# Shifted S5 kernel tables, gate stores from ScalarE, and tied TensorE steps in a hybrid S5 / SSD / DeltaNet layer

## The chip, the cores and the metric

The program runs on one core of one Trainium2 chip. The metric is the device time of one execution in microseconds (us), the median of several runs on fast executions. The core has five engines with queues of their own: TensorE (PE in the profile; its weight loads are PEld), VectorE (DVE), ScalarE (ACT), GpSimd (POOL) and SyncE (SP). Each queue is worked in order: an instruction that waits holds up all that stand behind it on its engine. Transfers between memory and the on-chip buffers are issued by a queue (here nearly all by SP) and carried by 16 DMA engines.

## The reference

One layer with 1024 channels is applied to 128 context tokens and 256 latent tokens with shared weights. The kernel keeps activations transposed, 8 blocks of 128 channels by 384 tokens.

```python
h = rmsnorm(x, g0) * (1 + sc1) + sh1                     # sh, sc, gate = silu(cond) @ ada_w + ada_b
x = x + 0.5 * g1 * swiglu(h, ffn_wi[0], ffn_wo[0])       # first feed-forward, width 2816
h = rmsnorm(x, g1) * (1 + sc2) + sh2
proj = h @ w_in          # u_s5, z, xbc, dt, qkv, beta, a, dn_gate, gate_raw
# S5: diagonal complex recurrence per channel group, forward and backward, then a GLU
# SSD: Mamba-2 chunks of 128;  DeltaNet: chunked delta rule with a triangular inverse
merged = sum(sigmoid(gate_raw[i]) * branch[i] for i in range(3))
x = x + g2 * (merged @ w_out)
h = rmsnorm(x, g2) * (1 + sc3) + sh3
x = x + 0.5 * g3 * swiglu(h, ffn_wi[1], ffn_wo[1])
y = rmsnorm(x, final_g)
```

## The kernel before

All dense products are done in three passes. `split_w` (L279) loads a 512 KB weight block into `wraw` (three buffers), ScalarE rounds it to `whi` (L284), VectorE makes the remainder `wlo` (L285; two buffers each), and `mm3` (L288) runs, for each of 8 slices of the contraction, `whi` with the high part of the activation, `whi` with its low part and `wlo` with the high part: 24 matmuls of 384 columns for one block of 128 outputs.

The order on every engine is made at build time by a scheduler that plays the program through with its own times; the program text and the limits of buffers bound it. `tc.issue_after(x)` sets a lower bound: what is written under it is issued after instruction `x`.

The stages in order of time are: the first feed-forward (`ffn(0)`), in whose gaps the modulation rows (`ada_rest`) and the S5 tables (`s5_tables`) are made; the mixer; the second feed-forward. In the mixer:

- Four S5 input blocks (`dense_in(0..3)`) are multiplied with the unnormalised activation `xh`, `xl`. `rstd_bcast` (L320) sums squares on TensorE (L326), takes the root on VectorE, and multiplies it back out to all partitions (L333); ScalarE copies this to `rb` (L337). Everything after needs `rb`: the blocks' scaling (L748), the normalised activation `hh`, `hl` (`modnorm`, L366), and a block of small scalars (`wsm`).
- The S5 input goes through memory (`dU`) and comes back in chunks of eight tokens as `UU` (eight transfers, L769). `chunk_inputs(b)` (L772), for b = 0 to 7, loads a table `sw` and runs 8 small matmuls (L778) whose results ScalarE copies to `Ss` (L781 to L783).
- Eighteen blocks of the DeltaNet and SSD inputs follow (`dense_in`, `conv`), then the z gate in four weight loads (L876 to L878, 36 matmuls of 256 columns for three tiles each half).
- The S5 scan over chunks, 31 steps on VectorE (L825, L826, L829), starts when all of `Ss` stands, and its end is copied to `Hc` (L952 to L955).
- The S5 output (L975) takes for each j of 8 the tables `ew` (one 512 KB transfer, L962) and, for even j, `tw`. `tw` holds for each of eight positions s the S5 kernel shifted by 16 s columns. Memory holds the kernel unshifted as `dK`, rows of 240 columns, and eight transfers of 64 KB (L966) read eight shifted pieces. `sw`, `ew`, `tw` and two later tiles share three buffers (`w4`).
- `gates()` (L1007) yields the dense filler of the inverse part: 16 gate blocks whose tanh is stored to `dM` (L1012), and steps of `ada_cols` (L234), each half of which loads modulation columns (L241) and multiplies them (L243). It is woven with `inv16` (L921), which inverts 16 by 16 blocks on VectorE and passes them through memory (`U`, L929; `dI`, L942), and then with the inverses and recurrences.

Of the kernel before, what the change touches and what calls it, by code (L numbers as in the profile page):

```python
# [10 lines left out]
F32 = mybir.dt.float32  # L11
# [9 lines left out]
P = 128  # L21
# [17 lines left out]
GK = ()  # L39
NSC = 0  # L40
NEARLY = (0, 0, 2, 1, 2)
NYF = 3
# [10 lines left out]
TW = T + 2  # L53
# [87 lines left out]
def tile_hybrid(ctx: ExitStack, tc: tile.TileContext, a, o):  # L141
    nc = tc.nc
# [136 lines left out]
    def split_w(dram, nk, w=P, into=None):  # L279
# [6 lines left out]
        return hi, lo  # L286

    def mm3(pt, w, xh, xl, k0, nk, start, stop):  # L288
        hi, lo = w
        for k in range(nk):  # L290
            PE.matmul(pt, hi[:, k, :], xh[k0 + k], start=start and k == 0, stop=False)  # L291
            PE.matmul(pt, hi[:, k, :], xl[k0 + k], start=False, stop=False)  # L292
            PE.matmul(pt, lo[:, k, :], xh[k0 + k], start=False, stop=stop and k == nk - 1)  # L293

# [25 lines left out]
    def rstd_bcast(acc, width, copy=True, ps=None, rest=(), root=False):  # L320
# [11 lines left out]
        for t in range(3):  # L332
            PE.matmul(pb[:, t * P:t * P + P], y[:, t:t + 1].to_broadcast([P, P]), ident, start=True, stop=True)  # L333
        if not copy:
# [114 lines left out]
    dE = dram.tile([8, P, 2, 2, 2, P], F32, name="dE")  # L449
    dK = dram.tile([4, 2, 4, 32, 240], F32, name="dK")  # L450
    dU = dram.tile([512, 8, 48], F32, name="dU")
# [97 lines left out]
    def s5_tables(sp, b, bb, craw, pq, pb):  # L549
# [50 lines left out]
        S.copy(kc[:, 128:240], pf[:, 16:128])  # L600
        nc.sync.dma_start(out=dK[b % 4, b // 4].rearrange("g i c -> (g i) c"), in_=kc)
        yield
# [92 lines left out]
    def mixer(es, xv, acc, xh, xl, sc):  # L695
# [46 lines left out]

        pts = [dense_in(m, xh, xl, TW) for m in range(2)]
        rb = rstd_bcast(acc, D)
        for m in range(4):
            pt = pts[m] if m < 2 else dense_in(m, xh, xl, TW, psD if m < 3 else psC)
            ur = t2("ur", None)[:, 0:T]
            V.tensor_tensor(ur, pt[:, 0:T], rb, op=ALU.mult)  # L748
            bu = shifts(pt)
            us = wk.tile([P, 8, 48], F32, name="us", tag="sgate", bufs=NSG)  # L750
            for e, s0, s1 in HALVES:
                S.activation(us[:, :, s0 // 8:s1 // 8], ur[:, s0:s1].rearrange("p (c s) -> p s c", s=8),
                             AF.Identity, bias=bu[:, e:e + 1])
            nc.sync.dma_start(out=dU[m * P:m * P + P], in_=us)
# [34 lines left out]
        for which, tokt in ((1, ktok), (0, qtok), (2, vtok)):  # L789
            for m in range(4):  # L790
# [6 lines left out]
                if which < 2:  # L797
                    sq = raw
                    S.activation(sq, pt.rearrange("p a b -> p (a b)"), AF.Square)
                    V.tensor_reduce(ss[:, which, :, m], sq.rearrange("p (a b) -> p a b", b=P), axis=AX.X, op=ALU.add)  # L800
                if which == 0:
                    chunk_inputs(2 * m)
                    chunk_inputs(2 * m + 1)
        V.tensor_scalar(ss, ss, EPS, None, op0=ALU.add)
# [153 lines left out]
        gsh, gsl = blocks("gsh", 4, FR), blocks("gsl", 4, FR)  # L958
        dk = dK.rearrange("b q g i c -> b i (q g) c")
        for j in range(8):  # L960
            ew = w4("ew").rearrange("p q (r g) c -> p q r g c", r=2)
            nc.sync.dma_start(out=ew, in_=dE[j])  # L962
            if j % 2 == 0:
                tw = w4("tw")
                for s in range(8):
                    nc.sync.dma_start(out=tw[16 * s:16 * s + 16].rearrange("p q g c -> p (q g) c"),  # L966
                                      in_=dk[j // 2, 0:16, :, 16 * (7 - s):16 * (7 - s) + P])
                pt = psB([P, 4, P])
# [38 lines left out]
        def gates():  # L1007

            cols = chain(*(ada_cols(s, lambda: wk.tile([P, 256], F32, name="arow")) for s in TSEC))
            for n in (2, 1):  # L1010
                for m in range(KD):
                    nc.sync.dma_start(out=dM[m, n], in_=gate(n, m))  # L1012
                    next(cols, None)
                    yield
# [138 lines left out]
        for d in range(2):  # L1153
            G.memset(hss[d], 0.0)
            for g in range(2):
                nc.sync.dma_start(out=hss[d][H2[g], 256 * g:256 * g + 256], in_=a["hssd"][H2[g], d])
        gram = []
# [267 lines left out]
```

## Time and profile before

| | before |
|---|---|
| median of 3 runs | 1155.57 us (1152.33 to 1156.07) |
| profiled execution | 1160.1 us, of which its span on the core 1158.3 us |
| mean granted TensorE clock of the span | 0.979 of full |
| busy: PE, DVE, ACT, POOL | 1096.5, 817.0, 473.0, 150.5 us |
| first feed-forward; mixer; second feed-forward (read from the trace) | to about 349 us; to about 850 us; to the end |

A wait in the trace stands in brackets behind the instruction that waited, with the one that released it. The granted clock is 1.0 at 2.4 GHz and 0.5 at 1.2 GHz, so a stretch at 0.86 spent part of its time at the lower level.

### The profile page before, as it was taken

The numbers are of one execution on the slowest core, as the hardware profiler recorded it, in microseconds if no ns is written. First come the engines' busy times: TensorE is split into PE (matmuls) and PEld (weight loads), VectorE is DVE, ScalarE is ACT, GpSimd is POOL, SyncE is SP. The second block draws the span as 40 slices with busy tenths as digits, with TensorE's granted clock in tenths as the row PEclk, the third lists the DMA queues.
The fourth block names the chain that finished last, engine by engine and source line by source line (L and its number), as shares of the span: only waits on it lengthen the run. The fifth ranks groups of instructions, "written<-read, shape, count | busy, mean of one in ns | idle before, by whom it ended". The sixth has DMA issues, their size and how long they took to land.

```text
span 1158.3 us, 19080 instructions
## 1 busy us (share of the span) xinstructions
PE 1096.5 (95%) x7192; PEld 1034.4 (89%) x7192; DVE 817.0 (71%) x1704; ACT 473.0 (41%) x858; POOL 150.5 (13%) x138
## 2 busy tenths in 40 slices
PE   4889999999999999999889999999999999999996
PEld 2689989999998999888678888999899999999996
DVE  4679998899966658985534569786776984455554
ACT  5343322333455587745333232233444432234341
POOL 0000000000000101034334546214400000000000
PEclk9999999999999799999899999999999999999998
DMA  9786767566574635347865442346754644544342
GB/s 351 274 255 205 223 217 253 194 204 199 155 242 139 152 116 158 111 124 231 236 188 178 126 124 80 103 139 189 232 184 149 202 127 114 146 123 127 105 123 82
DMA packets 107340, 199.19 MB, mean 172 GB/s; under 512 B 35056, under 2 KB 61936, under 8 KB 106992
## 3 DMA queue, kind: packets, MB, share of 16 engines
q1 hardware_dynamic: 107248, 197.98, 55.5%
q8 instruction: 56, 0.92, 0.3%
q14 instruction: 36, 0.29, 0.1%
HBM read 175.56 MB, written 22.38 MB: 171 GB/s over the span
## 4 chain that ended last, share of the span: by engine, by line
PE 74%; DVE 10%; DMA 5%; ACT 3%; issue 3%; POOL 2%; SPq 2%; DVEq 0%; POOLq 0%; ACTq 0%
PE ps_d L293 21%; PE ps_d L291 20%; PE ps_d L292 20%; DVE wlo L285 3%; ACT whi L284 1%; DVE sc L825 1%; DVE Ss L829 1%; PE ps_s L778 1%; PE ps_c L1040 1%; PE ps_m L221 1%; PE ps_m L856 1%; DMA tw<-dK 1%; DMA cb<-in_condr_dram 1%; DMA wraw<-in_win_dram 1%; DMA ew<-dE 1%
## 5 line engine op out<-in xcount | busy, mean ns | idle before, releaser
L284 ACT CAST whi<-wraw 128x1024 fp32r<-128x1024 f32 (+3 forms) x247 | 227.9, 924 | 445.9 <-PE ps_d L292 289.6
L285 DVE TENSOR_TENSOR wlo<-wraw,whi 128x1024 fp32r<-128x1024 f32 (+3 forms) x247 | 276.5, 1120 | 123.9 <-ACT whi L284 122.5
L291 PE MATMUL ps_d<-hh,whi 128*128 128x384 f32 x696 | 242.5, 350 | 18.5 <-ACT whi L284 15.3
L293 PE MATMUL ps_d<-hh,wlo 128*128 128x384 f32 x696 | 244.5, 352 | 4.2 <-DVE wlo L285 3.9
L292 PE MATMUL ps_d<-hl,whi 128*128 128x384 f32 x696 | 242.3, 348 | 0.4 <-DVE hl L379 0.4
L291 PEld LDWEIGHTS ps_d<-hh,whi 128*128 128x128 f32 x696 | 134.6, 194 | 27.9 <-ACT whi L284 18.8
L293 PEld LDWEIGHTS ps_d<-hh,wlo 128*128 128x128 f32 x696 | 134.5, 193 | 12.7 <-DVE wlo L285 8.8
L292 PEld LDWEIGHTS ps_d<-hl,whi 128*128 128x128 f32 x696 | 134.6, 193 | 3.1 <-DVE hl L379 1.3
L293 PE MATMUL ps_d<-gh,wlo 128*128 128x384 f32 x352 | 120.1, 341 | 4.3 <-DVE wlo L285 4.3
L291 PE MATMUL ps_d<-xh,whi 128*128 128x386 f32 x352 | 120.1, 341 | 0.0
L293 PE MATMUL ps_d<-xh,wlo 128*128 128x386 f32 x352 | 119.9, 341 | 0.0
L291 PE MATMUL ps_d<-gh,whi 128*128 128x384 f32 x352 | 119.7, 340 | 0.0
L292 PE MATMUL ps_d<-gl,whi 128*128 128x384 f32 x352 | 119.3, 339 | 0.0
L292 PE MATMUL ps_d<-xl,whi 128*128 128x386 f32 x352 | 119.1, 338 | 0.0
L271 DVE SCALAR_TENSOR_TENSOR ajunk<-araw,cb 128x1024 bf16<-128x1024 f32 x80 | 97.7, 1221 | 1.5 <-ACT cb L263 1.4
L293 PEld LDWEIGHTS ps_d<-gh,wlo 128*128 128x128 f32 x352 | 66.5, 189 | 5.9 <-DVE wlo L285 5.4
L291 PEld LDWEIGHTS ps_d<-gh,whi 128*128 128x128 f32 x352 | 66.7, 190 | 0.5 <-ACT whi L284 0.3
L292 PEld LDWEIGHTS ps_d<-gl,whi 128*128 128x128 f32 x352 | 66.8, 190 | 0.0
L292 PEld LDWEIGHTS ps_d<-xl,whi 128*128 128x128 f32 x352 | 66.6, 189 | 0.0
L291 PEld LDWEIGHTS ps_d<-xh,whi 128*128 128x128 f32 x352 | 66.4, 189 | 0.0
L293 PEld LDWEIGHTS ps_d<-xh,wlo 128*128 128x128 f32 x352 | 66.3, 188 | 0.0
L854 POOL TENSOR_TENSOR Atri<-smalls,dahl 128x512 fp32r<-128x512 f32 x36 | 41.9, 1183 | 80.2 <-DVE dahl L762 70.2
(465 smaller groups left out, 1747.6 us busy)
## 6 DMA issues: line engine op xcount, KB each, us to landing
wraw<-in_wi_dram SPq DMA_DIRECT2D x88, 512.0 KB
araw<-in_ada_dram SPq DMA_DIRECT2D x56, 512.0 KB
wraw<-in_win_dram SPq DMA_DIRECT2D x50, 512.0 KB
wraw<-in_wo_dram SPq DMA_DIRECT2D x32, 384.0 KB
wraw<-in_wo_dram SPq DMA_DIRECT2D x32, 320.0 KB
wraw<-in_ada_dram SPq DMA_DIRECT2D x16, 512.0 KB
wraw<-in_wbr_dram SPq DMA_DIRECT2D x32, 256.0 KB
dM<-sgate SPq DMA_DIRECT2D x24, 192.0 KB
```

Of the source, the lines that this page charges most:

```text
L221: PE.matmul(pt[32 * g:32 * g + 32, :], c32[:, k, :], raw[:, j, :], start=q < 2, stop=q >= 2, tile_position=(0, 32 * g))
L271: V.scalar_tensor_tensor(junk, raw, 1.0, cb[:, e], op0=ALU.mult, op1=ALU.mult, accum_out=t[:, b, e:e + 1])
L284: S.copy(hi, raw)
L285: V.tensor_tensor(lo, raw, hi.bitcast(F32), op=ALU.subtract)
L291: PE.matmul(pt, hi[:, k, :], xh[k0 + k], start=start and k == 0, stop=False)
L292: PE.matmul(pt, hi[:, k, :], xl[k0 + k], start=False, stop=False)
L293: PE.matmul(pt, lo[:, k, :], xh[k0 + k], start=False, stop=stop and k == nk - 1)
L778: PE.matmul(pt[:, ri, g], sw[:, ri, g], UU[:, 4 * b + g], start=True, stop=True)
L825: V.tensor_tensor(t[w][:, 0:nx], bc(mu[:, w], [P, nx, 2, 32], 1), bc(hv, [P, nx, 2, 32], 2), op=ALU.mult)
L829: V.tensor_tensor(sv_, sv_, t[0][:, 0:nx, ri], op=ALU.add)
L854: G.tensor_tensor(A, bc(INCL[d], [P, 4, P], 1), bc(dahl[:, w, x, 12 * d + c0:12 * d + c0 + 4], [P, 4, P], 2), op=ALU.mult)
L856: PE.matmul(pt.rearrange("p h i -> p (h i)"), strict[:, d], A.rearrange("p h i -> p (h i)"), start=d + w == 0, stop=d + w == 2)
```

## The change

Five edits are made.

1. **S5 kernels stored shifted.** `s5_tables` stores each kernel table with four transfers that read overlapping windows of the tile, so that memory (`dT`) holds all eight shifts. `tw` is then one transfer of 512 KB.
2. **Gate stores on ScalarE.** The 16 stores of `dM` in the loop over n, m are issued from ScalarE's queue.
3. **Chunk inputs tied.** Pairs of `chunk_inputs` are called after the DeltaNet blocks (1,2), (1,3), (0,0), (0,1), and not before the last matmul of the block they follow. Before, they stood after (0,0) to (0,3) with no tie.
4. **Fourth S5 block tied.** `dense_in(2)` and `dense_in(3)` are called before the scaling loop, and block 3 is issued after the last matmul of `rstd_bcast`.
5. **Section steps spaced.** `ada_cols` advances with every second gate block, so that eight of its sixteen steps fall to the last loop of `gates()`. The `hss` load is made in two transfers instead of four.

```diff
+CHUNKS = ((1, 2), (1, 3), (0, 0), (0, 1))
...
-        nc.sync.dma_start(out=dK[b % 4, b // 4].rearrange("g i c -> (g i) c"), in_=kc)
+        for g in range(4):
+            v = kc[32 * g:32 * g + 16, 0:P]
+            v = bass.AP(tensor=v.tensor, offset=v.offset, ap=[list(v.ap[0]), [16, 8], [1, P]])
+            nc.sync.dma_start(out=dT[b % 4].rearrange("(s i) q g c -> i s q g c", s=8)[:, ::-1, b // 4, g], in_=v)
...
         rb = rstd_bcast(acc, D)
+        root = last_mm[0]
+        pts.append(dense_in(2, xh, xl, TW))
+        with tc.issue_after(root):
+            pts.append(dense_in(3, xh, xl, TW, psC))
...
-                if which == 0:
-                    chunk_inputs(2 * m)
-                    chunk_inputs(2 * m + 1)
+                if (which, m) in CHUNKS:
+                    c = CHUNKS.index((which, m))
+                    with tc.issue_after(last_mm[0]):
+                        chunk_inputs(2 * c)
+                        chunk_inputs(2 * c + 1)
...
-                for s in range(8):
-                    nc.sync.dma_start(out=tw[16 * s:16 * s + 16].rearrange("p q g c -> p (q g) c"),
-                                      in_=dk[j // 2, 0:16, :, 16 * (7 - s):16 * (7 - s) + P])
+                nc.sync.dma_start(out=tw, in_=dT[j // 2])
...
-                    nc.sync.dma_start(out=dM[m, n], in_=gate(n, m))
-                    next(cols, None)
+                    nc.scalar.dma_start(out=dM[m, n], in_=gate(n, m))
+                    if m % 2 == 0:
+                        next(cols, None)
```

On TensorE, at the mixer's start, from the column sums of the norm (`ones`, `acc`) over the multiplication of its root (`ident`, `ry`) to the first chunk inputs (`UU`, `sw`), the order was this; `ps_c_3618` is the fourth S5 block, `ps_d_3579` the third, and `ps_d_3818`, `ps_d_3864` the first two DeltaNet blocks.

```order
L326 MATMUL ps_m_3536<-ones_81,acc_3045 128x1 x3
L291 MATMUL ps_d_3579<-xh_3049,whi_3582 128x386
L292 MATMUL ps_d_3579<-xl_3051,whi_3582 128x386
L291 MATMUL ps_c_3618<-xh_3049,whi_3621 128x386
...
L333 MATMUL ps_m_3557<-ident_76,ry_3542 128x128 x3
...
L291 MATMUL ps_d_3864<-hh_3658,whi_3867 128x384
L778 MATMUL ps_s_4050<-UU_3803,sw_4048 128x48 x8
L292 MATMUL ps_d_3818<-hl_3660,whi_3821 128x384
```

Now the fourth block (`ps_c_3618`) stands behind the root, and the first chunk inputs behind the third DeltaNet block (`ps_d_3934`):

```order
L329 MATMUL ps_m_3560<-ones_81,acc_3069 128x1 x3
L294 MATMUL ps_d_3587<-xh_3073,whi_3590 128x386
...
L296 MATMUL ps_d_3587<-xh_3074,wlo_3591 128x386
L336 MATMUL ps_m_3581<-ident_76,ry_3566 128x128 x3
L294 MATMUL ps_c_3618<-xh_3073,whi_3621 128x386
...
L296 MATMUL ps_d_3934<-hh_3682,wlo_3938 128x384
L788 MATMUL ps_s_3982<-UU_3827,sw_3980 128x48 x8
L788 MATMUL ps_s_3999<-UU_3827,sw_3997 128x48 x2
```

The root was multiplied out after 44 matmuls behind the column sums and now after 24; the chunk inputs began 44 matmuls into the normalised blocks and now begin after 72.

On VectorE, at the end of the S5 scan (the `Ss` updates), the order was this; `zt` and `aT` belong to the z gate and the DeltaNet stage.

```order
L825 TENSOR_TENSOR sc0_4769<-mu_112,Ss_3812 128x64
L866 SCALAR_TENSOR_TENSOR zt_5242<-th_5243,ps_d_5147 128x256
L285 TENSOR_TENSOR wlo_5732<-wraw_5729,whi_5731 128x1024
L829 TENSOR_TENSOR Ss_3812<-Ss_3812,sc0_4769 128x32
L829 TENSOR_TENSOR Ss_3813<-Ss_3813,sc0_4769 128x32
L913 TENSOR_TENSOR aT_5306<-ps_m_5333,segd_5324 128x256
```

Now the scan ends ahead of `wlo_5115`, the remainder of the second z weight:

```order
L838 TENSOR_TENSOR sc0_4793<-sc0_4793,sc1_4794 128x64
L841 TENSOR_TENSOR Ss_3836<-Ss_3836,sc0_4793 128x32
L841 TENSOR_TENSOR Ss_3837<-Ss_3837,sc0_4793 128x32
L286 TENSOR_TENSOR wlo_5115<-wraw_5112,whi_5114 128x1024
L878 SCALAR_TENSOR_TENSOR zt_5154<-th_5155,ps_d_5067 128x256
```

The scan's last step moved from behind the second gate weight to ahead of the second z weight, five weights earlier.

On SP, in the S5 output stage, weights (`wraw`) stood between pieces of `tw` and gate stores:

```order
L966 DMA tw_5540<-dK_106 16x8x128 x3
L918 DMA dL_108<-Lc_5386 128x4x64
L966 DMA tw_5540<-dK_106 16x8x128 x2
L962 DMA ew_5564<-dE_105 128x1024
L929 DMA U16_5640<-dL_108 24x16x16 x4
L1012 DMA dM_110<-sgate_5852 128x384
L282 DMA wraw_6085<-in_win_dram 128x1024
```

Now the same stretch reads:

```order
L973 DMA ew_5583<-dE_105 128x1024
L242 DMA wraw_5920<-in_ada3_dram 128x1024
L976 DMA tw_5585<-dT_106 128x1024
L973 DMA ew_5600<-dE_105 128x1024
...
L941 DMA U16_5646<-dL_108 24x16x16 x4
L1166 DMA hss_5967<-in_hssd_dram 64x2x256 x2
L283 DMA wraw_6058<-in_win_dram 128x1024
```

Seven of eight `tw` issues and all gate stores of this loop left the queue here, and three weight loads stand ahead of the `U` loads.

## Rows read from the trace of the kernel before

**Rows 1.** Stretches: PE, PEld, DVE, ACT, POOL busy us (instructions), clock, DMA share, GB/s

```profile
100.00:350.00 250.00, 242.53 (x1576) 236.13 (x1575) 222.19 (x380) 92.19 (x152) 1.45 (x3) 0.99 0.67 211
350.00:400.00 50.00, 46.16 (x240) 44.15 (x239) 33.88 (x93) 23.02 (x49) 4.84 (x4) 0.86 0.57 151
400.00:450.00 50.00, 50.00 (x339) 49.83 (x338) 28.91 (x58) 44.28 (x123) 2.24 (x3) 1.00 0.50 144
...
445.50:518.30 72.80, 67.96 (x451) 62.69 (x451) 71.28 (x210) 39.68 (x88) 13.24 (x11) 1.00 0.41 114
...
500.00:525.00 25.00, 22.22 (x153) 18.69 (x151) 19.67 (x60) 10.21 (x18) 11.83 (x12) 1.00 0.48 149
525.00:550.00 25.00, 23.79 (x202) 20.73 (x202) 13.38 (x35) 11.47 (x20) 9.89 (x10) 1.00 0.81 232
550.00:575.00 25.00, 19.75 (x177) 16.70 (x178) 15.34 (x67) 5.93 (x10) 7.51 (x6) 0.86 0.83 235
575.00:600.00 25.00, 20.39 (x162) 17.95 (x161) 8.07 (x14) 9.33 (x17) 6.26 (x7) 0.93 0.84 228
```

**Rows 2.** PE's timeline, 357 to 489 us (start, us, instruction, idle before)

```profile
357.81 0.72 PE L326 MATMUL ps_m<-ones,acc 128*128 128x1 f32 x6
...
366.49 0.83 PE L333 MATMUL ps_m<-ident,ry 128*128 128x128 f32 x6
...
374.66 0.45 PE L291 MATMUL ps_d<-hh,whi 128*128 128x384 f32 x1 [2.21 <-ACT whi L284]
...
387.97 1.96 PE L778 MATMUL ps_s<-UU,sw 128*128 128x48 f32 x16 [0.98 <-DMA UU<-dU]
...
488.62 0.39 PE L878 MATMUL ps_d<-wlo,hh 128*128 128x256 f32 x1 [1.06 <-DVE wlo L285]
```

**Rows 3.** DVE's and ACT's timelines at the root

```profile
362.21 0.16 DVE L309 SCALAR_TENSOR_TENSOR ry<-rsq,ry 128x3 f32<-128x3 f32 x1
...
367.36 0.48 ACT L337 COPY rb<-ps_m 128x384 f32<-128x384 f32 x1 [2.98 <-PE ps_m L333]
```

**Rows 4.** The scan's updates by line (ns min/median/max), and remainders among its steps

```profile
L829 DVE TENSOR_TENSOR Ss<-Ss,sc x62: 201/256/1080, 445.5 to 518.3; 128x32 f32<-128x32 f32 x32, 128x64 f32<-128x64 f32 x30
...
L285 DVE TENSOR_TENSOR wlo<-wraw,whi 128x1024 fp32r<-128x1024 f32 x12 | 14.6, 1220 | 0.0
```

**Rows 5.** PE's waits, 488 to 606 us (total us, times, longest)

```profile
PE ps_d L291 <- ACT whi L284: 5.1, 2, 2.6
PE ps_d L293 <- DVE wlo L285: 3.5, 5, 1.8
PE ps_d L243 <- DMA wraw<-in_ada_dram: 1.5, 1, 1.5
...
PE ps_s L975 <- DMA tw<-dK: 1.4, 2, 0.9
```

**Rows 6.** SP's timeline, 551 to 560 us

```profile
551.60 1.22 SPq L282 DMA_DIRECT2D wraw<-in_win_dram  x1
...
556.07 4.02 SPq L966 DMA_DIRECT2D tw<-dK  x8
```

**Rows 7.** ACT's timeline at the first missing weight

```profile
556.62 1.04 ACT L284 CAST whi<-wraw 128x1024 fp32r<-128x1024 f32 x1 [6.99 <-DMA wraw<-in_win_dram]
```

**Rows 8.** DVE's waits, 488 to 606 us

```profile
DVE T L934 <- DMA U<-dL: 10.5, 2, 6.4
```

**Rows 9.** SP's issues by line (ns min/median/max)

```profile
L966 SPq DMA_DIRECT2D tw<-dK x32: 303/426/697, 442.7 to 559.8; - x32
...
L601 SPq DMA_DIRECT2D dK<-tK x8: 373/407/488, 105.5 to 319.3; - x8
...
L1012 SPq DMA_DIRECT2D dM<-sgate x16: 326/354/1650, 517.3 to 652.6; - x16
```

**Rows 10.** SP's waits, 500 to 660 us

```profile
SPq L1012 <- ACT sgate L999: 17.1, 7, 6.1
```

**Rows 11.** The chain of waits, 586 to 594 us (start, us, what)

```profile
586.32 7.14 DMA wraw<-in_win_dram
```

More of the change, by code (lines that the diff above doesn't have):

```diff
@@ L286, in split_w @@
         return hi, lo
+    last_mm = [None]
     def mm3(pt, w, xh, xl, k0, nk, start, stop):
@@ L292, in mm3 @@
             PE.matmul(pt, hi[:, k, :], xl[k0 + k], start=False, stop=False)
-            PE.matmul(pt, lo[:, k, :], xh[k0 + k], start=False, stop=stop and k == nk - 1)
+            last_mm[0] = PE.matmul(pt, lo[:, k, :], xh[k0 + k], start=False, stop=stop and k == nk - 1).ins
     def rsqrt(y, x, root=False):
@@ L332, in rstd_bcast @@
         for t in range(3):
-            PE.matmul(pb[:, t * P:t * P + P], y[:, t:t + 1].to_broadcast([P, P]), ident, start=True, stop=True)
+            last_mm[0] = PE.matmul(pb[:, t * P:t * P + P], y[:, t:t + 1].to_broadcast([P, P]), ident, start=True, stop=True).ins
         if not copy:
@@ L449, in tile_hybrid @@
     dE = dram.tile([8, P, 2, 2, 2, P], F32, name="dE")
-    dK = dram.tile([4, 2, 4, 32, 240], F32, name="dK")
+    dT = dram.tile([4, P, 2, 4, P], F32, name="dT")
     dU = dram.tile([512, 8, 48], F32, name="dU")
@@ L744, in mixer @@
         rb = rstd_bcast(acc, D)
+        root = last_mm[0]
+        pts.append(dense_in(2, xh, xl, TW))
+        with tc.issue_after(root):
+            pts.append(dense_in(3, xh, xl, TW, psC))
         for m in range(4):
-            pt = pts[m] if m < 2 else dense_in(m, xh, xl, TW, psD if m < 3 else psC)
+            pt = pts[m]
             ur = t2("ur", None)[:, 0:T]
@@ L958, in mixer @@
         gsh, gsl = blocks("gsh", 4, FR), blocks("gsl", 4, FR)
-        dk = dK.rearrange("b q g i c -> b i (q g) c")
         for j in range(8):
@@ L1154, in mixer @@
             G.memset(hss[d], 0.0)
-            for g in range(2):
-                nc.sync.dma_start(out=hss[d][H2[g], 256 * g:256 * g + 256], in_=a["hssd"][H2[g], d])
+        for g in range(2):
+            nc.sync.dma_start(out=hs4[H2[g], :, 256 * g:256 * g + 256], in_=a["hssd"][H2[g]])
         gram = []
```

## The prediction

> **What bounds the kernel now.** I read the view of stretches first: for each it gives what every engine was busy, the granted clock and the DMA share. TensorE is the bound nearly everywhere. In the first feed-forward it is busy 242.53 of 250 us [rows 1], so work added there to SP or the DMA engines has cover. The sum of TensorE's work is not changed, so the change can only win back what TensorE idles, or spends at 1.2 GHz, in the stages that it moves. Two stages lose: 350 to 400 us with 3.84 us idle and a mean clock of 0.86, and 500 to 600 us, where 2.78 + 1.21 + 5.25 + 4.61 = 13.85 us are idle and the clock falls to 0.86 and 0.93 in the last two quarters [rows 1]. A mean of 0.86 over 25 us is 3.5 us of full-speed time lost, 0.93 is 1.75 us.
>
> Then the timeline at the first losing stage. The root's result is ready on VectorE at 362.21 + 0.16 = 362.4 us, but TensorE multiplies it out only at 366.49, and ScalarE has `rb` from 367.36 [rows 2, 3]. All of `hh`, `hl` follows from `rb`, and TensorE waits 2.21 us at 374.66 and once more, 0.98 us, for `UU` at 387.97 [rows 2].
>
> Third, between the two stages, the S5 scan. It runs from 445.5 to 518.3, and in that time VectorE is busy 71.28 of 72.8 us [rows 1, 4]: the scan stage is VectorE's, with TensorE idle 72.8 - 67.96 = 4.8 us.
>
> Fourth, the waits from 488 to 606 us. The largest are weights that come late: 5.1 us for `whi`, 3.5 for `wlo`, 1.5 for `ada` weights, 1.4 for `tw` [rows 5]. A weight issued by SP at 551.60 lets ScalarE start only at 556.62, another takes 7.14 us to land [rows 6, 7, 11]. SP is at `tw` pieces and the DMA engines are 0.81 to 0.84 busy there [rows 1, 6].
>
> **The change part by part.** The sum is made against the profiled execution, 1160.1 us, of which 1158.3 are the span; the median of the runs is 1155.57, 4.5 lower, and I take the difference that I find from both alike.
>
> *Fourth block behind the root, and chunk inputs later.* I place a mark at 488.62, where TensorE gets the second z weight [rows 2], and work out when it gets there now. TensorE's pace is (366.49 - 357.81 - 0.59) / 44 = 0.184 us per block matmul, 0.59 being the column sums up to the next start. With 24 of them ahead of the root instead of 44, TensorE is free for it at 362.8, and the root is ready at 362.4: no stall worth counting. One weight cast of ScalarE, about 1.05 us, stands ahead of the `rb` copy, so `rb` comes at about 363.9, 3.5 us earlier. `hh`, `hl` are made by VectorE and ScalarE at their own pace and move with it. TensorE's first normalised blocks still start at 372, since the S5 and scalar blocks ahead of them are the same work, but most of the 2.21 us wait and the slow stretch after it go. I put the end of the first two DeltaNet blocks at 381.5.
>
> A loss is added there. Before, the first chunk inputs ran while the third block's weight was cast. Now the third block stands directly behind both, which end three matmuls apart, and TensorE waits for one cast (1.04 us, as in [rows 7]) and one remainder (1.22 us [rows 4]): 2 us. From 383.5, 22 + 24 + 24 + 24 = 94 block matmuls (17 us), 64 chunk matmuls (1.96 us for 8, so 15.7 us) [rows 2] and some 3 us of transposes lead to a scan start at 419 us, against 445.5.
>
> From there VectorE sets the pace. By its order the scan's stretch has one remainder, six `zt` and sixteen DeltaNet products less than before and four convolution taps and the key norms more; by their durations that is 3 us less, so 68 to 70 us: the scan ends at 489, and the second z weight's remainder, which the order puts right behind it, is ready at 490.4. TensorE's own work in between, 288 block matmuls (53 us) and an estimated 10 us of transposes and z matmuls by that pace, takes 63 us: it waits about 7 us for VectorE in small pieces. So the mark moves from 488.6 to 490.4: **1.8 us lost** although the scan starts 26 us earlier. Bounds: if the scan starts at 424 because the third block's wait brings the lower clock, 6 lost; if VectorE were no limit, 419 + 63 = 482, 6 gained. I take the middle term since VectorE's 98% busy is a row.
>
> *From the mark to 600 us.* Before, the scan was still running for 30 us behind the mark; now it is over, and what it delayed goes with it. `tw` is 4 issues instead of 32 of 0.426 us each [rows 9]: 12 us of SP's queue, most of it between 528 and 560. Sixteen gate stores leave SP with 0.354 us each [rows 9] and with the 17.1 us that SP waited for their tanh with weights queued behind [rows 10]. Half the `ada` steps, 8 loads of 512 KB, move behind 600 us, where the DMA engines have room. Of the waits I let go 5.1, 1.5 and 1.4, and of the 3.5 about 2, with 3.5 us of the 5.25 us of clock: 13.5 us. The waits of VectorE on `U`, 10.5 us [rows 8], stay, since the chain through memory is the same, and 1.5 us come new, as `ew` now holds its buffers until the scan ends. **12 us gained.** Bounds: 3 (only `tw` and `ada` go, 1.4 + 1.5) and 17 (all but 2 of 13.85 + 5.25).
>
> The Trainium skill, in "DMA: Bandwidth & Descriptors", section "Issuing engines are not separate DMA queues", says that issuing from several engines only saves the time on the sequencer, usually small beside the transfer. By that sentence the gate stores are worth 16 x 0.354 = 5.7 us of SP and no more; the row on the waits says that the queue behind them is worth three times that. The sum goes by the row.
>
> *ScalarE's side.* Sixteen issues of 0.33 to 1.65 us [rows 9] are 5.7 us at the median, on an engine busy 6 to 11 us of each 25 [rows 1]; the cover is its idle time. A store must wait for the tanh ahead of it and for a completion count, and behind it stand weight casts. I take **1 us lost**; bounds 0 and the rival below.
>
> *`dT` stores and `hss`.* 24 issues more at 0.407 us [rows 9] are 9.8 us of SP over 215 us of a stage that TensorE bounds: 0, with 2 lost if a weight comes late. Two `hss` issues less: 0. *Later `ada` steps* bring no work: 0, bounds 2 lost and 1 gained.
>
> Sum: -1.8 + 12 - 1 = 9.2 us faster. 1160.1 - 9 = 1151 for the profiled execution, and 1155.6 - 9 = **1147 us** for the median.
>
> **The rivals.** (a) *VectorE takes it all.* The earlier scan makes VectorE the bound from 419 on, the mark falls 6 us back, and the S5 output then waits for `Hc` and its tables, so that only 6 to 8 us come back later: 1155, no change. For it speaks VectorE's 71.28 of 72.8; against it the 50 - 28.91 = 21 us that VectorE idles between 400 and 450 us, which an earlier scan can fill [rows 1].
>
> (b) *ScalarE blocks: slower.* A gate store on ScalarE waits for the completion of an earlier transfer, and the weight casts behind it wait along. With transfers of 7.14 us [rows 11] ten of the sixteen stores hold it for 2.5 us each, and where a hold is longer than the slack of a block (4.4 us for 24 matmuls less the 1.04 us cast, 3.3 us with what is already late) TensorE idles and drops to 1.2 GHz. Price: 10 x 1.2 us of idle and 4 us of clock, 16 us, against 9 + 1 gained: 1161. Against it: the transfer waited for was issued eight transfers earlier, and with `tw` and `ada` gone the DMA engines are freer.
>
> (c) *Everything clears.* All idle time and clock of 500 to 600 us goes but 2 us, and the mark is 6 us earlier: 17 + 6 = 23, 1133.
>
> (d) *The change does not do what it says*: the shorter queue lets SP issue earlier but the DMA engines, not SP, set the landing, so weights land as before; 4 us from the rest, 1152.
>
> **How the numbers follow.** About 0.3% (3.5 us) can be told from no change: faster is below 1152.1, slower above 1159. Forecast 0.60, its own range 1140 to 1152; (a) 0.13, (b) 0.11, (c) 0.10, (d) 0.06. Faster: 0.58 of the forecast's 0.60, 0.10 of (c), 0.02 of (d): 0.70. Slower: 0.11 of (b) and 0.02 of (a): 0.13. Same: 0.17. The range that holds 8 in 10 goes from 1137, into (c), to 1157, over (a) and short of (b).
>
> **What would show it.** Right: `rb` near 364 instead of 367.36; the scan's first update near 419 and its last near 489 with VectorE over 95% busy between; the second z weight near 490; between there and the first inverse products no wait above 2 us for `whi`, the clock at 1.0, and SP without blocks of `tw`. The step on ScalarE is wrong if its stores stand before idle time that ends in a late `whi`. The sum is wrong if the mark lies beyond 496, or if the idle time of the inverse stage is above 8 us.

## The result, and the profile after

The changed kernel takes **1143.76 us** (median of 4 runs, 1141.98 to 1148.1) beside 1155.82 for the kernel before: a ratio of **0.9894, 95% interval 0.9863 to 0.9926**. The prediction was 1147 us. Measured once more beside other kernels, the ratio was 0.9877 (0.9851 to 0.9904). The profiled execution has a span of 1146.3 us against 1158.3; both took about 4.3 us more than the median of their kernel (1148.1 and 1160.1 us).

The stretches of the changed kernel, which answer to [rows 1] (columns as there; the last row is the scan):

```profile
100.00:350.00 250.00, 240.95 (x1567) 234.37 (x1566) 220.53 (x377) 92.02 (x151) 1.46 (x3) 0.99 0.70 214
350.00:400.00 50.00, 46.38 (x280) 44.38 (x279) 38.34 (x100) 30.49 (x70) 5.39 (x4) 1.00 0.59 154
...
500.00:525.00 25.00, 23.80 (x227) 21.03 (x227) 12.81 (x35) 7.15 (x14) 16.81 (x16) 1.00 0.73 233
525.00:550.00 25.00, 25.00 (x188) 22.00 (x188) 15.09 (x63) 10.88 (x18) 10.20 (x11) 1.00 0.76 227
550.00:575.00 25.00, 23.29 (x156) 21.39 (x154) 14.00 (x38) 9.55 (x19) 3.56 (x3) 1.00 0.71 194
575.00:600.00 25.00, 22.90 (x202) 19.81 (x204) 13.27 (x15) 8.21 (x12) 17.13 (x15) 0.93 0.57 182
...
421.60:487.00 65.40, 60.06 (x359) 58.44 (x358) 62.82 (x201) 40.64 (x98) 4.25 (x3) 0.97 0.34 105
```

Both losing stages have changed. From 350 to 400 us TensorE idles as long as before (50 - 46.38 = 3.6 us), but its clock is 1.00 in place of 0.86, by an estimate from the mean clock 50 x 0.14 = 7.0 us. From 500 to 600 us the idle time falls from 13.85 to 1.20 + 0 + 1.71 + 2.10 = 5.0 us and the clock loss from 5.25 to 1.75. The scan's stretch is still VectorE's, 62.82 of 65.40 us busy (96%).

TensorE's timeline, which answers to [rows 2] (start, us, instruction, idle before):

```profile
363.45 0.83 PE L336 MATMUL ps_m<-ident,ry 128*128 128x128 f32 x6
...
375.73 0.44 PE L294 MATMUL ps_d<-hh,whi 128*128 128x384 f32 x1 [1.18 <-ACT whi L285]
...
391.07 2.33 PE L788 MATMUL ps_s<-UU,sw 128*128 128x48 f32 x20
...
460.61 0.66 PE L296 MATMUL ps_d<-hh,wlo 128*128 128x384 f32 x1 [3.12 <-DVE wlo L286]
...
488.40 0.39 PE L890 MATMUL ps_d<-wlo,hh 128*128 128x256 f32 x1
```

ScalarE's timeline at the root, which answers to [rows 3]:

```profile
364.43 0.48 ACT L340 COPY rb<-ps_m 128x384 f32<-128x384 f32 x1
```

The root is multiplied out 3.0 us sooner, the wait of 2.21 us is now 1.18, and the wait for `UU` is gone. The mark, the second z weight, lies at 488.40 us, before at 488.62: up to there nothing is won. In the scan's stretch TensorE now idles 65.40 - 60.06 = 5.3 us; its longest wait there is one for VectorE, 3.12 us at 460.61.

The scan's updates, VectorE's substitution that ends in the inverse's input `W`, SP's stores of `dL` ahead of it, and the first inverse products, by line (ns min/median/max, first and last start in us), which answer to [rows 4] and to the two rows of the kernel before behind them:

```profile
L841 DVE TENSOR_TENSOR Ss<-Ss,sc x62: 199/223/298, 421.3 to 487.0; 128x32 f32<-128x32 f32 x32, 128x64 f32<-128x64 f32 x30
...
L946 DVE TENSOR_TENSOR T<-U,W x30: 150/276/824, 540.7 to 561.0; 96x1 f32<-96x1 f32 x2, 96x4 f32<-96x4 f32 x2, 96x9 f32<-96x9 f32 x2, 96x16 f32<-96x16 f32 x2
...
L930 SPq DMA_DIRECT2D dL<-Lc x6: 370/370/377, 509.5 to 535.3; - x6
...
L1050 PE MATMUL ps_s<-X,Lm x96: 218/218/267, 574.3 to 683.7; 64*64 64x64 f32 x96
```

The same stores and substitution in the kernel before, its first inverse products, and the products of the S5 output:

```profile
L918 SPq DMA_DIRECT2D dL<-Lc x6: 370/380/382, 514.1 to 546.8; - x6
...
L934 DVE TENSOR_TENSOR T<-U,W x30: 152/255/840, 553.1 to 573.0; 96x1 f32<-96x1 f32 x2, 96x4 f32<-96x4 f32 x2, 96x9 f32<-96x9 f32 x2, 96x16 f32<-96x16 f32 x2
...
L1040 PE MATMUL ps_s<-X,Lm x96: 218/219/268, 588.2 to 700.0; 64*64 64x64 f32 x96
...
L975 PE MATMUL ps_s<-ew,Hc x128: 272/273/311, 522.7 to 568.3; 128*48 128x128 f32 x128
```

The S5 output in the changed kernel:

```profile
L984 PE MATMUL ps_s<-ew,Hc x128: 272/273/311, 491.0 to 541.1; 128*48 128x128 f32 x128
```

The S5 output starts 31.7 us earlier. The last `dL` store goes out 11.5 us earlier, the substitution starts 12.4 us earlier, and the first inverse product starts at 574.3 us for 588.2. So 13.9 us are won between the mark and the inverse, and 12.0 are left at the end.

TensorE's waits from 490 to 610 us, which answer to [rows 5] (total us, times, longest):

```profile
PE ps_s L1050 <- DMA X<-dI: 1.6, 1, 1.6
PE ps_d L294 <- ACT whi L285: 0.9, 1, 0.9
...
PE ps_d L296 <- DVE wlo L286: 0.6, 1, 0.6
```

VectorE's wait that answers to [rows 8], and the issues that answer to [rows 9]:

```profile
DVE T L946 <- DMA U<-dL: 5.9, 2, 3.8
```

```profile
L976 SPq DMA_DIRECT2D tw<-dT x4: 320/390/423, 418.5 to 529.1; - x4
...
L607 SPq DMA_DIRECT2D dT<-tK x32: 326/428/2069, 104.1 to 319.5; - x32
...
L1021 ACTq DMA_DIRECT2D dM<-sgate x16: 326/326/384, 521.0 to 631.9; - x16
```

The waits for `whi` and `wlo` are nearly gone (0.9 and 0.6 us), as forecast; so is nearly half of VectorE's wait for `U`, which the prediction had let stand. What stood before the inverse is best read in the chain of waits. A part of it in the kernel before (start, us, what):

```profile
528.87 5.76 DMA tw<-dK
...
539.98 6.76 DMA ew<-dE
...
554.25 3.19 DMA U<-dL
```

And in the changed kernel, over the same part of the work:

```profile
493.66 1.03 ACT Hc L967
...
496.21 3.22 DMA dZ<-zt
...
499.98 7.01 DMA dZ<-zt
...
511.34 3.48 DMA dZ<-zt
```

Before, the way to the inverse led over the tables of the S5 output and the strings of issues on SP between them. Now it leads over the z gate's transfers (`dZ`, 3.22 + 7.01 + 3.48 us), and no transfer of those tables lies on it.

### The profile page after: what moved, and what is told of

Read it like the earlier page. It is cut to its first block, busy times and chain, and to the rows that moved or that the text cites. A ratio compares the mean times of both kernels' runs of the same rounds, so it can differ in the third digit from the quotient of the medians.

```text
span 1146.3 us, 19067 instructions
## 1 busy us (share of the span) xinstructions
PE 1091.6 (95%) x7192; PEld 1028.2 (90%) x7192; DVE 810.6 (71%) x1704; ACT 470.9 (41%) x856; POOL 148.1 (13%) x138
## 4 chain that ended last, share of the span: by engine, by line
PE 72%; DVE 13%; DMA 5%; ACT 4%; issue 4%; POOL 1%; SPq 1%; DVEq 0%; ACTq 0%; POOLq 0%
PE ps_d L296 20%; PE ps_d L294 20%; PE ps_d L295 19%; DVE wlo L286 3%; ACT whi L285 2%; DMA dZ<-zt 1%; DMA cb<-in_condr_dram 1%; PE ps_c L1050 1%; DVE sc L837 1%; DVE cv L687 1%; DMA wraw<-in_win_dram 1%; PE ps_m L868 1%; PE ps_m L222 1%; PE ps_s L788 1%; DVE nt L379 1%
## 5 line engine op out<-in xcount | busy, mean ns | idle before, releaser
L296 PE MATMUL ps_d<-hh,wlo 128*128 128x384 f32 x696 | 241.5, 348 | 4.2 <-DVE wlo L286 4.2
L295 PE MATMUL ps_d<-hl,whi 128*128 128x384 f32 x696 | 239.3, 344 | 0.4 <-DVE hl L382 0.4
## 6 DMA issues: line engine op xcount, KB each, us to landing
wraw<-in_wo_dram SPq DMA_DIRECT2D x32, 384.0 KB
```

The costliest lines, as they stand in the source:

```text
L296: last_mm[0] = PE.matmul(pt, lo[:, k, :], xh[k0 + k], start=False, stop=stop and k == nk - 1).ins
```

## The experiments

Twelve more kernels ran in three groups, each beside the kernel before. "Less" is the changed kernel with the edit named taken back; in the rows with the S5 output free, `Hc` is not taken from the scan (last section of experiments). The two middle columns are TensorE's idle time plus its clock loss (length times 1 less the mean clock) in us, from each trace; the last two are the end of the scan and the start of the inverse, counted from the column sums of the norm, because these came anywhere from 352.3 to 358.1 us from one execution to the next. The windows of the middle columns do not move with them, so differences of 1 or 2 us there mean little.

| kernel | ratio to before (95%) | 350-400 | 500-600 | scan ends | inverse starts |
|---|---|---|---|---|---|
| before | 1 | 3.8 + 7.0 | 13.9 + 5.2 | 160.5 | 230.4 |
| changed | 0.9894 (0.9863-0.9926) | 3.6 + 0 | 5.0 + 1.7 | 128.9 | 216.2 |
| changed, again | 0.9877 (0.9851-0.9904) | 3.6 + 0 | 4.0 + 0 | 128.9 | 214.9 |
| less: gate stores | 0.9918 (0.9896-0.9940) | 2.9 + 1.5 | 4.9 + 1.8 | 127.8 | 214.9 |
| less: shifted kernels | 0.9917 (0.9895-0.9938) | 3.1 + 1.5 | 6.6 + 3.5 | 129.7 | 221.2 |
| less: spaced columns | 0.9924 (0.9904-0.9943) | 2.8 + 1.5 | 9.2 + 5.3 | 127.6 | 213.2 |
| less: whole order | 0.9993 (0.9965-1.0021) | 6.0 + 7.0 | 9.0 + 5.2 | 163.1 | 230.5 |
| before with the order alone | 0.9969 (0.9951-0.9988) | 3.1 + 3.5 | 14.8 + 8.5 | 129.5 | 226.3 |
| less: chunk inputs early | 1.0022 (1.0003-1.0041) | 4.5 + 7.0 | 12.1 + 6.7 | 155.6 | 230.6 |
| less: fourth block | 0.9929 (0.9903-0.9955) | 3.9 + 3.5 | 6.8 + 0 | 131.8 | 219.3 |
| chunk inputs late, S5 output free | 0.9969 (0.9948-0.9990) | 4.2 + 5.0 | 8.0 + 6.7 | 152.4 | 226.3 |
| changed, S5 output free | 0.9900 (0.9877-0.9923) | 3.1 + 1.5 | 3.1 + 3.5 | 128.0 | 218.7 |
| less: tie of the chunk inputs | 0.9943 (0.9923-0.9964) | 4.8 + 7.0 | 3.8 + 1.7 | 139.0 | 221.9 |
| chunk inputs one block earlier | 0.9909 (0.9880-0.9939) | 3.9 + 7.0 | 3.3 + 5.0 | 136.6 | 219.2 |

Two things stand out from 500 to 600 us. With all queue edits, a scan that is over by 139 us goes with a loss of 4.0 to 8.3 us, one that ends at 152 us or later with 14.2 to 18.8. With no queue edit the loss is 23.3 us although the scan is over by 129.5.

### Gate stores back on SP

```diff
-                    nc.scalar.dma_start(out=dM[m, n], in_=gate(n, m))
+                    nc.sync.dma_start(out=dM[m, n], in_=gate(n, m))
```

> The changed kernel with one edit taken back: the sixteen gate stores are issued by SP again. Theory (SP's queue): before, SP waited 17.1 us for the tanh behind these stores with weights queued behind them, and TensorE's waits for whi and wlo from 488 to 606 us were 5.1 and 3.5 us; these come back, with part of the clock: 1143.8 + 6 = 1150, with waits of SP at the gate stores of over 10 us and TensorE idle 6 us or more from 500 to 600 us. Rival (TensorE's order): the gain is that the scan is over when the inverse stage begins, and SP has time to wait: 1144 to 1145. Rival (ScalarE pays): the stores cost ScalarE as much as they save: 1142 to 1143.

The ratio is 0.0024 to 0.0041 above the changed kernel's two, 3 to 5 us, with an interval that overlaps that of the first and barely touches that of the second. SP's waits from 490 to 660 us begin with

```profile
SPq L1021 <- ACT sgate L1008: 30.1, 9, 9.3
```

SP stands 30.1 us for the tanh, more than the 17.1 of [rows 10], and yet the stage from 500 to 600 us loses no more than in the first trace of the changed kernel. So what waits on SP here is, as it seems, mostly not late. The 3 to 5 us could not be found in one stretch; the execution that was profiled is, at 1146.31 us, one of the fastest of this kernel and shorter than the first one profiled of the changed kernel (1148.1), so the traces hardly hold the difference.

### Shifted kernels taken back

```diff
-                nc.sync.dma_start(out=tw, in_=dT[j // 2])
+                for s in range(8):
+                    nc.sync.dma_start(out=tw[16 * s:16 * s + 16].rearrange("p q g c -> p (q g) c"),
+                                      in_=dk[j // 2, 0:16, :, 16 * (7 - s):16 * (7 - s) + P])
```

> The changed kernel with one edit taken back: the S5 kernels are stored unshifted (8 stores) and each of the four tables is read in eight pieces. Theory (SP's queue): 28 issues more of 0.426 us, 12 us of SP's queue, in a stage that has 4 to 5 us of idle TensorE left; the waits for tw and for weights behind them come back in part: 1143.8 + 4 = 1148. Rival (TensorE's order): the tables are asked for ahead of the S5 output, which now lies beside z products that need no weight from SP: 1144 to 1145. Rival (the 24 stores more cost the first feed-forward): 1141 to 1143.

The eight stores of the tables come back with it. It lost 3 to 5 us, as the theory had it, again with an interval that overlaps that of the changed kernel's first measurement, and the inverse starts 5 to 6 us later. The first feed-forward shows the price of the 24 stores more: without them

```profile
100.00:350.00 250.00, 242.53 (x1577) 236.31 (x1577) 219.49 (x375) 92.18 (x151) 1.45 (x3) 0.99 0.68 212
```

7.5 us of 250 idle, with them 9.05 (first fence). All three traces with eight stores (before, this one, the order alone) have 7.5, the others 8.7 to 9.4: about 1.5 us.

### Spaced columns taken back

```diff
-                    if m % 2 == 0:
-                        next(cols, None)
+                    next(cols, None)
```

> The changed kernel with one edit taken back: a step of the section columns after every gate block. Theory (SP's queue): 8 loads of 512 KB come back into the stage from 500 to 600 us with 24 GB more each 100 us on the DMA engines that were 0.81 to 0.84 busy there: 1143.8 + 2 = 1146. Rival (DMA engines, not SP, set the landing): the gain is mostly this edit, 1143.8 + 7 = 1151, with the DMA share back above 0.8. Rival (TensorE's order): 1143 to 1144.

3.5 to 5 us are lost, between the two forecasts (8 loads of 512 KB over 100 us are 42 GB/s; the 24 in the text is a slip). The interval overlaps that of the changed kernel's first measurement and begins where that of the second ends. The stage from 500 to 600 us loses 14.5 in place of 4 to 7, although the inverse itself starts no later: TensorE has run out of other work and waits 6.0 us once, for `Lm`. The DMA share there was 0.76, 0.80, 0.72 and 0.46, so the rival's sign (over 0.8 throughout) is not seen.

### TensorE's order taken back, and alone

Taken back are the edits on the fourth block and the chunk inputs, with their ties; alone means these two on the kernel before. The diffs are those of the next section, together.

> The changed kernel with TensorE's order taken back: the fourth S5 block and the chunk inputs are placed as in the kernel before, without ties; the other edits stay. Theory (SP's queue): the scan starts near 445 us and ends near 518 again, the mark (second z weight) is where it was, and the stage behind keeps what the shorter queues gave it: 1143.8 - 2 + 2 for the scan's end that the S5 output waits for, 1142 to 1146. Rival (TensorE's order is the gain): the 30 us of scan that stood behind the mark delay everything behind it again: 1143.8 + 9 = 1153.

> The kernel before with one edit alone: fourth S5 block behind the root's matmul and chunk inputs ahead of the third and fourth DeltaNet blocks, tied; tables, stores and columns as before. Theory A (TensorE's order by itself is the gain: scan over by 490 us, root without its wait): 10 to 12 us faster than before, ratio 0.990 to 0.991. Theory B (order and the other edits need each other: the earlier S5 output then waits for tw pieces and weights in SP's queue): 4 to 6 us faster, ratio 0.995 to 0.9965, with waits for tw or whi of over 5 us from 490 to 600 us. Theory C (the blind sum: the order loses 2, the queues win): ratio 1.000 to 1.002.

These two runs carry the argument. Without the order the other edits are worth nothing that can be measured: 0.9993. Part of that is lost at the root: from 500 to 600 us this kernel has 4.9 us less of idle time and clock loss than the kernel before, but from 350 to 400 us it has 2.1 us more, since TensorE waits 2.86 us for `UU` there and not 0.98, and the z gate comes 2.6 us later (its first product with a remainder 129.5 us after the column sums, before 126.9). The order alone brings 0.31%. Together they bring 1.06 to 1.23%. The stretches from 350 and from 500 us, first with the order taken back, then with the order alone:

```profile
350.00:400.00 50.00, 44.04 (x223) 41.91 (x222) 31.71 (x90) 21.23 (x44) 5.01 (x4) 0.86 0.54 139
500.00:600.00 100.00, 91.03 (x721) 81.85 (x721) 61.95 (x173) 39.40 (x67) 38.17 (x36) 0.95 0.69 205
```

```profile
350.00:400.00 50.00, 46.92 (x275) 45.05 (x274) 37.71 (x96) 32.46 (x76) 5.39 (x4) 0.93 0.54 138
500.00:600.00 100.00, 85.17 (x675) 72.09 (x676) 47.20 (x140) 33.09 (x57) 37.07 (x35) 0.91 0.75 206
```

With the order alone the scan is over by 129.5 us after the column sums, and still the later stage loses more than before, 14.8 + 8.5 us. TensorE's longest wait there, and the stores and substitution:

```profile
PE ps_d L294 <- ACT whi L285: 6.0, 2, 3.6
```

```profile
L927 SPq DMA_DIRECT2D dL<-Lc x6: 370/380/383, 510.3 to 538.8; - x6
...
L943 DVE TENSOR_TENSOR T<-U,W x30: 150/257/567, 548.0 to 568.0; 96x1 f32<-96x1 f32 x2, 96x4 f32<-96x4 f32 x2, 96x9 f32<-96x9 f32 x2, 96x16 f32<-96x16 f32 x2
```

Weights are late again, and from the last `dL` store to the substitution it takes 9.2 us, in the changed kernel 540.7 - 535.3 = 5.4. Theory B has the sign right (a wait for `whi` of over 5 us) and its ratio nearly, 0.995 to 0.9965 against 0.9969, and theories A and C are outside the interval: with the scan early, the longer queue of SP holds back what the scan set free. With the order taken back the queue is short and the scan late, and the substitution starts as late as ever (549.3 us, 193.8 after the column sums; before 195.3).

### The two halves of the order

> The changed kernel with the chunk inputs alone put back behind the second set of DeltaNet blocks, untied; the fourth S5 block stays behind the root. The scan then starts at 440 to 445 us and ends near 515 again, but the root's result is early. Theory (the end of the scan decides): most of the 11.5 us that the whole order is worth is lost, 1143.8 + 8 = 1152, and the loss lies behind 490 us. Rival (the root decides): the clock from 350 to 400 us stays at 0.97 to 1.00 and only 3 us are lost, 1147.

```diff
-                if (which, m) in CHUNKS:
-                    c = CHUNKS.index((which, m))
-                    with tc.issue_after(last_mm[0]):
-                        chunk_inputs(2 * c)
-                        chunk_inputs(2 * c + 1)
+                if which == 0:
+                    chunk_inputs(2 * m)
+                    chunk_inputs(2 * m + 1)
```

> The changed kernel with the fourth S5 block alone put back to where it was, untied; the chunk inputs stay early. The root's multiplication waits behind 20 block matmuls again, rb comes 9.6 us after the column sums in place of 6.3. Theory (the end of the scan decides): the scan starts 3 us later and 2 to 3 us are lost, 1146. Rival (the root decides): TensorE waits over 2 us behind the S5 blocks and has the lower clock there, 0.86 from 350 to 400 us: 1143.8 + 8 = 1152.

```diff
-        root = last_mm[0]
-        pts.append(dense_in(2, xh, xl, TW))
-        with tc.issue_after(root):
-            pts.append(dense_in(3, xh, xl, TW, psC))
...
-            pt = pts[m]
+            pt = pts[m] if m < 2 else dense_in(m, xh, xl, TW, psD if m < 3 else psC)
```

The chunk inputs carry it: with them late and untied the kernel is no faster than before (1.0022), 15 to 17 us worse than the changed one, twice the theory's 8. Taken back alone, the fourth block costs 4 to 6 us, between its two forecasts; with it taken back the 2.2 us wait behind the S5 blocks returns and the clock there is 0.93. The late chunk inputs lose in both stages. Their stretches, and TensorE's first chunk matmul:

```profile
350.00:400.00 50.00, 45.50 (x239) 43.87 (x239) 34.85 (x93) 26.64 (x57) 5.69 (x4) 0.86 0.47 117
500.00:600.00 100.00, 87.86 (x694) 78.78 (x693) 57.26 (x158) 38.39 (x65) 43.39 (x37) 0.93 0.66 196
```

```profile
380.66 0.39 PE L788 MATMUL ps_s<-UU,sw 128*128 128x48 f32 x2 [2.58 <-DMA UU<-dU]
```

Untied, the first pair slips ahead of the third DeltaNet block and meets the load of `UU`. The first product of the z gate with a remainder comes 133.2 us after the column sums, in the changed kernel 126.4: 6.8 us are lost ahead of it, and so not only behind 490 us, as the theory had it. Without the tie alone (next section) it comes at 133.6.

### The tie, and one block earlier

```diff
-                    with tc.issue_after(last_mm[0]):
-                        chunk_inputs(2 * c)
-                        chunk_inputs(2 * c + 1)
+                    chunk_inputs(2 * c)
+                    chunk_inputs(2 * c + 1)
```

> The changed kernel with the chunk inputs called at the same places, but not tied behind the last matmul of the block: the first pair moves ahead of the third DeltaNet block on TensorE, the last pair and the scan keep their places. Theory (the first pair runs into the load of UU, as the waits of 0.98, 2.86 and 2.58 us for UU in the kernels with the old place show, and TensorE falls to the lower clock there): the stage from 350 to 400 us has a clock of 0.86 to 0.93 and 3 to 7 us are lost, ratio 0.991 to 0.994. Rival (only the scan's place counts): 0.987 to 0.989.

```diff
-CHUNKS = ((1, 2), (1, 3), (0, 0), (0, 1))
+CHUNKS = ((1, 1), (1, 2), (1, 3), (0, 0))
```

> The changed kernel with each pair of chunk inputs one DeltaNet block earlier, tied as before: the first pair at about 383.5 us on TensorE, 4.5 us sooner, the scan's first step 4.5 us sooner. UU was there at 380.7 us in u_chunk, so no wait for it. Theory (VectorE has no room for more scan ahead, and the S5 output no longer waits): same time, 0.986 to 0.990. Rival (the scan's end still decides): 4 us faster, 0.984. Rival (UU is late): 0.992 with a wait of 2 us or more for UU.

Without the tie the stretch from 350 us has the clock of the kernel before again, and a wait of 2.9 us for `UU`:

```profile
350.00:400.00 50.00, 45.23 (x239) 43.60 (x238) 33.63 (x91) 25.06 (x52) 5.69 (x4) 0.86 0.51 124
```

```profile
PE ps_s L788 <- DMA UU<-dU: 2.9, 1, 2.9
```

It costs 6 to 8 us (0.9943), the theory's 3 to 7 or a little more; from 350 to 400 us alone it loses 8.2 us more than the changed kernel. Against the expectation the scan does not keep its place: it ends 10 us later (139.0 for 128.9). Yet from 500 to 600 us nothing is lost by that. One block earlier has the wait too (1.9 us) and the same clock of 0.86; its ratio of 0.9909 cannot be told from the changed kernel's, but gives no reason to go earlier. My figure for when `UU` is there, 380.7 us, was too early: it came from a trace whose column sums lie at 352.85 us, 5.3 us ahead of those of the changed kernel's trace. No version here beats the changed kernel.

### The S5 output freed from the scan

```diff
-            S.copy(hc[0:64, :, 1:16], Ss[ri][0:64, :, 0:15])
+            S.copy(hc[0:64, :, 1:16], UU[0:64, :, 0:15])
...
-            S.copy(hc[64:128, :, 16:47], Ss[ri][64:128, :, 46:15:-1])
+            S.copy(hc[64:128, :, 16:47], UU[64:128, :, 46:15:-1])
```

> The kernel with the chunk inputs late (u_chunk), in which the table Hc is filled from UU instead of the scan's result: the scan runs as before on VectorE, but the S5 output no longer waits for its end (its numbers are then other ones). Theory (what the late chunk inputs cost behind 490 us is the S5 output waiting for the scan's end): the stage from 500 to 600 us loses its 10 us of idle TensorE and lower clock, ratio 1.002 - 0.008 = 0.994. Rival (VectorE, busy with the scan until 508 us, delays remainders and zt itself): 1.000 to 1.003, as u_chunk. The 8 us lost from 350 to 400 us stay in both.

> The changed kernel with Hc filled from UU in the same way: the control for u_chunk_hc. Theory (the scan's end decides, and is early enough in the changed kernel): no gain, ratio 0.986 to 0.990 beside 0.988 for the changed kernel. Rival (to have the S5 output free is worth something always): 0.980.

These kernels leave out what the scan adds to the S5 output: `Hc` is filled from `UU`, which stands long before. The control gained nothing (0.9900). With late chunk inputs the freed S5 output brings 1.0022 - 0.9969 = 0.53%, 6 of the 15 to 17 us. The theory had 0.994, its rival 1.000 to 1.003, and the run lies between them. In that kernel

```profile
500.00:600.00 100.00, 92.05 (x752) 82.12 (x750) 56.72 (x158) 38.94 (x66) 44.01 (x40) 0.93 0.67 204
```

```profile
L928 SPq DMA_DIRECT2D dL<-Lc x6: 370/374/386, 511.8 to 538.8; - x6
```

TensorE is busy 4.2 us longer than with the S5 output bound (87.86 us), but the last `dL` store comes only 2.8 us sooner (183.1 us after the column sums for 185.9; changed kernel 177.2), and TensorE ends in a wait of 5.6 us for `X`. Of the 6 us some 2 lie from 350 to 400 us (11.5 us lost there with the S5 output bound, 9.2 with it free), where the S5 output has not begun. So the S5 output is one follower of the scan, worth some 4 us. That the rest of the loss behind the z gate is VectorE's own work towards the inverse, held up by the late scan on the same engine, is argued and not shown.

## Why the prediction was right, and where its reasons were not

**The number.** Forecast 9 us, measured 12 (1155.82 - 1143.76; 8.6 to 15.8 by the interval); the profiled execution's span came down by 12.0.

**Up to the mark: right.** `rb` was forecast at 363.9 and came at 364.43; the scan's start 419 (421.3) and end 489 (487.0), VectorE over 95% busy (96%); the mark 490.4 (488.40). The term of -1.8 was +0.2. The step that gives the third block a wait of 2 us was too high, 0.66 us in the trace; the end of the first two DeltaNet blocks, 381.5 in the forecast, was too early, 384.0.

**From the mark to 600 us: the size right, the reason wrong.** 12 us were forecast. In the forecast's own measure, idle time and clock loss from 500 to 600 us, 19.1 - 6.8 = 12.3 were won, and the inverse starts 13.9 us earlier. But the step booked them to the shorter queues (`tw`, gate stores, columns) and let the order stand for a loss of 1.8. The queue edits without the order gave 0.9993, the order without them 0.9969. Sums of edits priced one by one (0.07 + 0.31%) cannot give 0.9894 to 0.9877; 0.68 to 0.85%, 8 to 10 us, belong to the pair, with an uncertainty of about 0.4% from the three intervals. That 12 came out right is luck in part: the edits that it was booked to bring 0.8 us alone. The sentence that what the scan delayed "goes with it" was the right mechanism, but it had no term of its own.

**VectorE's waits on `U`, "10.5 us, stay": failed.** They fell to 5.9 us. The chain through memory is the same, but its last store came 11.5 us earlier and its loads stood behind fewer issues. Pieces of it (`U`, the substitution, the stores of `dI`) stand on the chain of waits ahead of the inverse in the kernel before and in the one with the order taken back; I had read these waits as idle time that costs nothing. The 1.5 us booked for `ew` were not seen: no wait of TensorE from 490 to 610 us is for `ew`.

**The gate stores: the row misread.** I took SP's wait of 17.1 us for three times the 5.7 us of issuing. Back on SP, the wait is 30.1 us and the price 3 to 5 us, at the edge of what the intervals tell from nothing. The Trainium skill, "DMA: Bandwidth & Descriptors", section "Issuing engines are not separate DMA queues", says that another issuing engine saves only sequencer time. Here the runs agree with it better than with my reading, 3 to 5 us beside 5.7. A wait on a queue is a price only where what stands behind it is late.

**The clock at the root: half of the cause.** The forecast saw one slow stretch, behind the fourth block's wait of 2.21 us. The trace of the kernel before has two, one behind that wait and ahead of `UU`, one behind the wait for `UU` and the first chunk inputs (columns as in [rows 1]):

```profile
376.00:383.00 7.00, 6.34 (x21) 5.46 (x21) 7.00 (x22) 5.49 (x16) 0.00 (x0) 0.55 0.99 222
...
390.00:397.00 7.00, 7.00 (x29) 7.00 (x29) 5.64 (x11) 4.05 (x10) 1.84 (x2) 0.52 0.46 148
```

Each lost about 3.4 us. With the fourth block taken back the wait of 2.20 us brings the first one alone; with the chunk inputs late, or untied, and the fourth block moved, there is one longer stretch behind the wait for `UU` (here chunk inputs late):

```profile
375.00:382.00 7.00, 6.59 (x21) 5.59 (x21) 7.00 (x22) 5.69 (x16) 0.00 (x0) 0.52 0.95 225
```

```profile
381.00:395.00 14.00, 14.00 (x59) 14.00 (x59) 8.07 (x10) 6.62 (x14) 5.69 (x4) 0.51 0.32 112
```

So neither edit of the order clears the 7 us by itself; with both as the changed kernel has them, 0 to 3.5 are left. Every trace in which TensorE waits for `UU` has a low clock from 350 to 400 us: 0.86 in five (before, the order taken back, chunk inputs late, no tie, one block earlier) and 0.90 in the sixth (chunk inputs late with the S5 output free). Those without that wait have 0.93 to 1.00.

**`dT` stores at 0: off by 1.5 us**, inside the bound of 2. **ScalarE's loss of 1 us** was not seen on TensorE: the issues take 0.326 us at the median, none above 0.384. The mechanism of rival (b) is there, but small. In the changed kernel two of the sixteen stores go out late behind their tanh, by 0.43 and 0.65 us; the longest hold of any trace here, 3.2 us, is in the run with the spaced columns taken back. The later of the two holds in the changed kernel, and the longest one:

```profile
567.69 0.49 ACT L1008 ACTIVATE sgate<-ps_d 128x384 f32<-128x384 f32 x1 [3.15 <-PE ps_d L296]
568.83 0.33 ACTq L1021 DMA_DIRECT2D dM<-sgate  x1
```

```profile
557.56 0.49 ACT L1008 ACTIVATE sgate<-ps_d 128x384 f32<-128x384 f32 x1
561.27 0.33 ACTq L1021 DMA_DIRECT2D dM<-sgate  x1
```

In neither trace does TensorE wait over 0.9 us for a weight's high part or remainder from 490 to 606 us, so the forecast's 16 us are far off. Rival (a) had the place right, VectorE 96% busy, but the mark did not fall back, and VectorE's later work came forward with the scan. Rival (c) went too far: 5.0 us of idle time and 1.75 of clock are left, and the mark is 0.2 us earlier in place of 6. Rival (d) is refuted by the 0.75 to 0.92% that the queue edits bring once the order is there (0.9969 to 0.9894 or 0.9877).

**Open.** Which of SP's issues the pair works through was argued from the traces and not tested by itself. Pairs of a queue edit and the order were not run, so the three queue edits' shares are known only from taking each away (3 to 5 us each, hardly clear of the noise). Each edit also moves the order on other engines a little, and where the 3 to 5 us of the gate stores lie was not found.

## What to carry to other kernels

When a serial scan on one engine fills a stage, ask what waits for its end, and what that same engine must do after it for the next stage: here bringing the scan forward paid there, and only when the transfers between were not queued behind others. Two edits that shorten different halves of one chain are to be tried together, since each alone can read as little or nothing (here 0.07 and 0.31%, together over 1%). A small block that depends on a round trip through memory can be better placed after one more large block than at the first moment its engine is free (the tie, 6 to 8 us).

## What the runs showed of the hardware

In four traces (the order taken back, chunk inputs late, no tie, one block earlier) a wait of 1.9 to 2.9 us ahead of the chunk matmuls of 48 columns was followed by one stretch at a granted clock of 0.50, the 1.2 GHz level, of about 14 us, a loss of 6.8 us and more than the wait itself; in a fifth (chunk inputs late with the S5 output free) the wait was 2.29 us and the loss 5.1. In the kernel before, 0.98 us there went with a loss of 3.4 us. The wait of 2.2 us behind the S5 blocks cost 3.4 us of clock in two traces (before, fourth block taken back) and none in a third (the order taken back, clock 1.00 from 372 to 385 us). Shorter waits in the changed kernel (1.18, 0.43, 0.66, 0.51, 0.54 us) left the clock at 1.00, though nearly the same waits with the longer SP queue (1.16, 0.46, 0.66, 0.50) had 0.93. What separates these the traces do not show.
